# Feed-forward gate and up projections by seven products per 2×2 block: an fp32 trunk of two layers on one core

## The chip, the core and the metric

The kernel runs on one core of a Trainium2 chip. The metric is device time in microseconds (us), as the median of three runs; the kernel before takes 1412.47 us (1409.63 to 1412.63). The core's engines are TensorE (PE; its weight loads are shown as PEld), VectorE (DVE), ScalarE (ACT), GpSimd (POOL) and SyncE (SP), which here only issues DMA transfers. Each engine executes its own instructions in program order and waits for others at semaphores.

## The reference

The program is a trunk of two residual layers for 512 tokens of width 1024, all in fp32. Layer 0 mixes tokens by retention, layer 1 by stick-breaking attention, and each is followed by the same kind of feed-forward part, which is what the change is about:

```
def swiglu(h, w_in, w_out):
    gate, up = jnp.split(h @ w_in, 2, axis=-1)
    return (jax.nn.silu(gate) * up) @ w_out

def reference(x, ...):
    for i in range(DEPTH):                              # DEPTH = 2
        h = rms_norm(x, mix_norm[i])
        x = x + (retention(h, ...) if i % N_MIXERS == 0 else stick_breaking(h, ...))
        x = x + swiglu(rms_norm(x, ffn_norm[i]), ffn_w_in[i], ffn_w_out[i])
    return x
```

`w_in` is 1024 x 5632 (gate and up of 2816 each) and `w_out` 2816 x 1024, per layer.

## The kernel before

**Layout.** Channels lie on the 128 partitions and the 512 tokens along the free dimension: `x` is eight tiles of 128x512 (k = 0..7). To keep fp32 accuracy every operand is held as a pair of high and low part, and every product is three matmuls, high by high, low by high, high by low (`split3`, L131 to L133 of the profile). The normalisation's row factor is applied behind the product; only the gain is multiplied into `xh`, `xl` (`norm_in`, L141, L142).

**Weights.** All weights come in blocks of 128x1024 fp32 (512 KB). The class `Weights` loads a block by a DMA from SP into `raw` (three buffers, three ahead), ACT copies it to the high part `wh` (L72) and DVE subtracts that from it to get the low part `wl` (L73), two blocks ahead of TensorE. PE takes the blocks in the order of the program's steps.

**Feed-forward.** A layer has 22 hidden tiles f of 128 channels, in two halves of 11. Tiles 0 and 1 are computed first in four chunks as the x tiles arrive (`ffn_first`, `ch_chunk`); then the column of mean squares (`stats_col`, L164 to L168, which needs `sq`, a running sum that POOL adds, L158) and a row form of the factor (`stats_row`, L175, L178). `ffn_tile(f)` for f from 2 computes gate and up as 8 x 3 matmuls of 512 columns each, one weight block for each; `ffn_act` then does gate by row (L502) on DVE, Silu (L504) on ACT, up by row and by that (L506, L507) on DVE, and the split into `hh` (L138, ACT) and `hl` (L139, DVE). Behind each half `ffn_out_chunk` multiplies the hidden tiles by `ffn_out`, and `add_x` adds the result to x (L233).

**Order of work.** The steps are issued in program order on each engine; the loads and splits of blocks run ahead of the step that takes them. All matmul results lie in one ring of eight PSUM banks, tag `mm`.

Of the kernel before, what the change touches and what calls it, by code (L numbers as in the profile page):

```python
# [26 lines left out]
HALF = FF // P // 2  # L27


class Weights:  # L30
# [3 lines left out]
    def __init__(self, nc, raw, split, load_ahead, split_ahead):  # L34
        self.nc, self.raw, self.split = nc, raw, split
        self.aps, self.raws, self.parts = [], {}, {}
        self.n_load = self.n_split = self.n_take = 0
        self.load_ahead, self.split_ahead = load_ahead, split_ahead
        self.hooks = {}
        self.first = None  # L40

    def load(self, n):
        nc = self.nc
        while self.n_load < min(n + self.load_ahead, len(self.aps)):
            for hook in self.hooks.pop(self.n_load, ()):
                hook()
            ap = self.aps[self.n_load]
            t = self.raw.tile([P, 1024], F32, tag="raw", name=f"raw{self.n_load}")
            w = ap.shape[-1]
            if self.n_load == 0 and self.first:  # L50
                for half, (ready, _) in zip((slice(0, w // 2), slice(w // 2, w)), self.first):
                    ready()
                    nc.sync.dma_start(t[:, half], ap[:, half])
            else:
                nc.sync.dma_start(t[:, :w], ap)
            self.raws[self.n_load] = (t, w)
            self.n_load += 1

    def advance(self, n):
        nc = self.nc  # L60
        self.load(n)
        while self.n_split < min(n + self.split_ahead, self.n_load):
            t, w = self.raws.pop(self.n_split)
            h = self.split.tile([P, 1024], F32R, tag="wh", name=f"wh{self.n_split}")
            l = self.split.tile([P, 1024], F32R, tag="wl", name=f"wl{self.n_split}")
            parts = [slice(0, w)]
            if self.n_split == 0 and self.first:
                parts = [slice(0, w // 2), slice(w // 2, w)]
            for i, part in enumerate(parts):
                if len(parts) > 1:  # L70
                    self.first[i][1]()
                nc.scalar.activation(h[:, part], t[:, part], AF.Copy)  # L72
                nc.vector.tensor_tensor(l[:, part], t[:, part], h[:, part].bitcast(F32), ALU.subtract)  # L73
            self.parts[self.n_split] = (h, l, w)
            self.n_split += 1

    def take(self):
        n = self.n_take
        self.advance(n + 1)
        self.n_take += 1  # L80
        return self.parts.pop(n)
# [810 lines left out]
```

## Time and profile before

| | us |
|---|---|
| median of three runs (range) | 1412.47 (1409.63 to 1412.63) |
| the profiled execution's own time | 1406.76 |
| its span, first to last instruction | 1405.1 |
| PE busy in it | 1381.4 (98%) |
| DVE, ACT, POOL busy | 723.8, 511.7, 204.1 |
| feed-forward of layer 0, gate and up from f = 3 / output | 92.5 + 119.6 / 60.4 + 60.5 |
| stick-breaking stage | 269.2 |

The profile is one execution, 5.7 us below the median of the three timed runs. Stages were found by following PE's instructions in time; a busy share is of the stretch named. An instruction's duration on PE overlaps the next one's, so PE's rate is read from the distance of starts. The clock granted to PE was 0.998 of full speed over the span, the higher of its two levels (2.4 GHz) nearly throughout.

### The profile page before, as it was taken

To read this page: it belongs to the slowest core of one execution; us is meant where nothing else is said; L and a number is where in the kernel's file an instruction comes from. 1 tells how busy PE (TensorE), PEld (TensorE's weight loads), DVE (VectorE), ACT (ScalarE), POOL (GpSimd) and SP (SyncE) were. 2 spreads that over 40 slices of the span, in tenths; PEclk is the share of its full clock that TensorE was granted. 3 is DMA by queue.
4 is the path that set the end of the run, shared out by engine and by line. 5 is a ranking of instruction groups with operands and counts; after the bars stand their busy time and mean duration, and the time that the engine had idled before them with its cause. 6 is when DMAs were issued, how large, how long until landed. Compare 5 with 4: busy or idle time off the path is not lost.

```text
span 1405.1 us, 16161 instructions
## 1 busy us (share of the span) xinstructions
PE 1381.4 (98%) x6331; PEld 1144.6 (81%) x6331; DVE 723.8 (52%) x915; ACT 511.7 (36%) x768; POOL 204.1 (15%) x262
## 2 busy tenths in 40 slices
PE   9999999999999999999999999988999999999999
PEld 7888888888888888888888887766888888888887
DVE  6555345364374443344434357789994443344432
ACT  5243233332353232223333356667653322223221
POOL 3000000000020000000002245676830000000000
PEclk9999999999999999999999999999999999999999
DMA  6322222213232323333234344335223333333332
GB/s 233 97 83 83 90 75 90 91 61 104 76 90 90 100 92 98 101 92 103 87 113 137 99 120 123 89 92 148 76 74 94 103 88 98 99 104 91 90 109 71
DMA packets 41948, 138.96 MB, mean 99 GB/s; under 512 B 5008, under 2 KB 5264, under 8 KB 41872
## 3 DMA queue, kind: packets, MB, share of 16 engines
q1 hardware_dynamic: 41872, 137.93, 32.5%
q8 instruction: 49, 0.80, 0.2%
q14 instruction: 27, 0.22, 0.1%
HBM read 125.33 MB, written 4.19 MB: 92 GB/s over the span
## 4 chain that ended last, share of the span: by engine, by line
PE 90%; DVE 3%; POOL 3%; issue 2%; ACT 1%; DMA 1%; SPq 0%; POOLq 0%; DVEq 0%; ACTq 0%
PE mm L131 29%; PE mm L133 29%; PE mm L132 29%; PE mm L698 1%; POOL sn L657 1%; POOL qf L603 1%; POOL w L664 1%; DVE wl L73 1%; PE mm L649 1%; PE mm L677 1%; DVE sn L663 1%; PE mm L405 0%; PE mm L650 0%; POOL w L657 0%; DMA raw<-in_ret_tok_dram 0%
## 5 line engine op out<-in xcount | busy, mean ns | idle before, releaser
L72 ACT ACTIVATE wh<-raw 128x1024 fp32r<-128x1024 f32 (+2 forms) x233 | 243.1, 1044 | 702.6 <-PE mm L132 410.5
L73 DVE TENSOR_TENSOR wl<-raw,wh 128x1024 fp32r<-128x1024 f32 (+2 forms) x233 | 285.8, 1227 | 278.9 <-ACT wh L72 277.9
L131 PE MATMUL mm<-xh,wh 128*128 128x512 f32 x832 | 324.4, 390 | 0.0
L133 PE MATMUL mm<-xh,wl 128*128 128x512 f32 x832 | 323.8, 389 | 0.0
L132 PE MATMUL mm<-xl,wh 128*128 128x512 f32 x832 | 323.7, 389 | 0.0
L133 PEld LDWEIGHTS mm<-xh,wl 128*128 128x128 f32 x832 | 156.2, 188 | 32.8
L131 PEld LDWEIGHTS mm<-xh,wh 128*128 128x128 f32 x832 | 156.2, 188 | 32.2
L132 PEld LDWEIGHTS mm<-xl,wh 128*128 128x128 f32 x832 | 156.2, 188 | 32.2
L132 PE MATMUL mm<-wl,xh 128*128 128x512 f32 x448 | 175.0, 391 | 1.5 <-DVE wl L73 1.4
L131 PE MATMUL mm<-wh,xh 128*128 128x512 f32 x448 | 175.1, 393 | 0.0
L133 PE MATMUL mm<-wh,xl 128*128 128x512 f32 x448 | 175.0, 391 | 0.0
L131 PE MATMUL mm<-hh,wh 128*128 128x512 f32 (+1 forms) x363 | 140.5, 387 | 0.0
L133 PE MATMUL mm<-hh,wl 128*128 128x512 f32 (+1 forms) x363 | 139.8, 385 | 0.0
L132 PE MATMUL mm<-hl,wh 128*128 128x512 f32 (+1 forms) x363 | 138.5, 382 | 0.0
L132 PEld LDWEIGHTS mm<-wl,xh 128*128 128x128 f32 x448 | 84.3, 188 | 19.7 <-DVE wl L73 2.8
L158 POOL TENSOR_TENSOR sq<-sq,sqt 128x512 f32<-128x512 f32 x28 | 43.1, 1538 | 391.4 <-issue 293.9
L133 PEld LDWEIGHTS mm<-wh,xl 128*128 128x128 f32 x448 | 84.1, 188 | 17.5
L131 PEld LDWEIGHTS mm<-wh,xh 128*128 128x128 f32 x448 | 84.2, 188 | 16.9
L506 DVE TENSOR_TENSOR us<-mm,row 128x512 f32<-128x512 f32 x44 | 30.4, 691 | 124.9 <-PE mm L133 124.9
L233 DVE TENSOR_TENSOR x<-mm,x 128x512 f32<-128x512 f32 x87 | 59.4, 686 | 57.9 <-PE mm L133 57.8
L133 PEld LDWEIGHTS mm<-hh,wl 128*128 128x128 f32 x363 | 68.1, 188 | 15.0
L132 PEld LDWEIGHTS mm<-hl,wh 128*128 128x128 f32 x363 | 68.1, 188 | 14.4
(114 smaller groups left out, 1589.0 us busy)
## 6 DMA issues: line engine op xcount, KB each, us to landing
raw<-in_ffn_in_dram SPq DMA_DIRECT2D x88, 512.0 KB, 3.5
raw<-in_ffn_out_dram SPq DMA_DIRECT2D x32, 512.0 KB, 3.5
raw<-in_ret_tok_dram SPq DMA_DIRECT2D x31, 512.0 KB, 3.5
raw<-in_sb_in_dram SPq DMA_DIRECT2D x24, 512.0 KB, 3.5
raw<-in_ret_ch_dram SPq DMA_DIRECT2D x16, 512.0 KB, 3.6
raw<-in_ret_o_dram SPq DMA_DIRECT2D x16, 512.0 KB, 3.5
kk<-kt SPq DMA_DIRECT2D x32, 256.0 KB, 4.4
raw<-in_ffn_out_dram SPq DMA_DIRECT2D x16, 384.0 KB, 3.2
```

Of the source, the lines that this page charges most:

```text
L72: nc.scalar.activation(h[:, part], t[:, part], AF.Copy)
L73: nc.vector.tensor_tensor(l[:, part], t[:, part], h[:, part].bitcast(F32), ALU.subtract)
L131: nc.tensor.matmul(ps, ah, bh, start=start, stop=False)
L132: nc.tensor.matmul(ps, ah, bl, start=False, stop=False)
L133: nc.tensor.matmul(ps, al, bh, start=False, stop=stop)
L158: nc.gpsimd.tensor_tensor(state["sq"], state["sq"], t, ALU.add)
L233: nc.vector.tensor_tensor(x[m], bank, x[m], ALU.add)
L506: nc.vector.tensor_tensor(us, up, row, ALU.mult)
L603: nc.gpsimd.tensor_tensor(QF[which, g][:, t], ss, mhalf, ALU.pow)
L649: nc.tensor.matmul(bank[:, :n], qs[:, ts], kk[:, 0, :n], start=True, stop=False)
L657: nc.gpsimd.affine_select(out=t[:, ts], in_=t[:, ts], compare_op=ALU.is_gt, fill=fill, base=0, pattern=[[-1, P]], channel_multiplier=1)
L663: nc.vector.tensor_tensor_scan(d, d, d, 1.0, ALU.mult, ALU.bypass)
```

## The change

For f = 2 to 21 gate and up are computed in groups of two tiles, ten groups per layer. In a group the weights are taken as a 2x2 matrix of blocks (even or odd k by gate or up) and x as a 2x2 matrix (even or odd k by the two halves of the tokens, `H1`, `H2`). Winograd's form of Strassen's product then needs seven products in place of eight. Each product takes one 128x1024 block (plain or a sum of blocks) and is 4 x 2 x 3 = 24 matmuls of 256 columns (`product`).

* The sums on the weight side are made as follows: `t3` = w22 + w12 and `t1` = w11 + w12 by a second, accumulating DMA that POOL issues onto a block already loaded (L116); `t2` = t1 + w22 and `t4` = t2 + w21 by DVE (L129). Blocks have two rings, `RAWS` 3 and `GROUP_RAWS` 6; ACT makes the high parts up to four items ahead, DVE the low parts with three buffers.
* The sums on the x side (`ffn_sums`) are made once per layer for each pair of k: two ACT copies (L595), four DVE operations of 256 columns (L598 to L601), and the split into `sxh` and `sxl` (128x1024; L241, L242).
* On the output side one product seeds another's bank: ACT copies a bank to a bank (L673, L689) or to SBUF (`p7`, L685) and DVE adds `p7` into a bank (L690) or to SBUF (`up`, L697). The first product of the next group (`ffn_group_open`, w11) is computed in the middle of a group, behind its third product.
* The tiles go in three passes of 8, 8 and 6 (`PASSES`), each with its output stage. The row factor of `up` moves from the hidden tiles to the output (`ffn_add`, two DVE operations in place of one). `stats_col` stands behind the second chunk instead of the fourth. PSUM has two rings of four banks, `mm` and `sd`.
* In the stick-breaking stage `sn` gets a buffer of its own for each j, where it had a ring of three, and `w3` has two buffers, where it had three.

```diff
-    def ffn_tile(f):
-        def go():
-            gate, up = psum(), psum()
-            ch_tile(gate)
-            ...
-            ch_tile(up)
-            ...
-            ffn_act(f, gate, up)
+    def product(bank, name, start):
+        h, l, _ = W.take()
+        ...
+        for p in range(KT // 2):
+            xh, xl = ff["ops"][p][name]
+            for s in range(2):
+                out = bank[:, s * (S // 2) : (s + 1) * (S // 2)]
+                nc.tensor.matmul(out, h[:, p, s], xh, ...)
+                nc.tensor.matmul(out, h[:, p, s], xl, ...)
+                nc.tensor.matmul(out, l[:, p, s], xh, ...)
+    def ffn_group_open(f):
+        def go():
+            a = bank("mm")
+            product(a, "11", True)
+            if f == 2:
+                stats_row(lambda: bank("mm"), ff["t"])
+                for i in range(2):
+                    ffn_up(i, ff["first"][2 * i + 1], ffn_gate(ff["first"][2 * i], None), None)
+            b = bank("sd")
+            nc.scalar.activation(b, a, AF.Copy)
+            ff["next"] = {"a": a, "b": b}
+    def ffn_group(f, n):
+        def go():
+            g = ff["group"] = ff["next"] if n == 0 else ff["group"]
+            if n == 0:
+                t = bank("mm")
+                product(t, "s3", True)
+                nc.scalar.activation(g["p7"], t, AF.Copy)
+            elif n == 1:
+                product(g["b"], "s2", False)
+                nc.scalar.activation(g["d"], g["b"], AF.Copy)
+                nc.vector.tensor_tensor(g["c"], g["b"], g["p7"], ALU.add)
+            elif n == 2:
+                product(g["a"], "12", False)
+                g["gate"] = ffn_gate(g["a"], H1)
+            elif n == 3:
+                product(g["d"], "s1", False)
+                nc.vector.tensor_tensor(g["up"], g["d"], g["p7"], ALU.add)
+            elif n == 4:
+                product(g["c"], "22", False)
+                ffn_up(f, g["up"], ffn_gate(g["c"], H2), H2)
+            else:
+                product(g["d"], "s4", False)
+                ffn_up(f, g["d"], g["gate"], H1)
...
+                for n in range(6):
+                    step(ffn_group(f, n), *([entry] if n == 0 and not own else []))
+                    if n == 2 and following:
+                        step(ffn_group_open(f + 2))
...
+                nc.sync.dma_start(t[:, :w], aps[0])
+                for ap in aps[1:]:
+                    nc.gpsimd.dma_start(t[:, :w], ap, accum_op=ALU.add)
...
-                w = sb["t"].tile([P, n], F32, tag=f"w{j}", name="w", bufs=3)
-                r = sb["t"].tile([P, S], F32, tag="sn", name="sn", bufs=3)
+                w = sb["t"].tile([P, n], F32, tag=f"w{j}", name="w", bufs=3 - (j == 3))
+                r = sb["t"].tile([P, n], F32, tag=f"sn{j}", name="sn", bufs=1)
```

**What moves on DVE at the start of layer 0's feed-forward part.** Before, DVE's rows from the last x tile to the first gate are these (`ms` is the mean-square column, `wl` a block's low part):

```order
L142 SCALAR_TENSOR_TENSOR xl<-x_81,gains,xh 128x512
L73 TENSOR_TENSOR wl_3230<-raw_3197,wh_3229 128x1024
L73 TENSOR_TENSOR wl_3260<-raw_3227,wh_3259 128x1024
L73 TENSOR_TENSOR wl_3290<-raw_3257,wh_3289 128x1024
L166 TENSOR_SCALAR ms<-mm 128x4
L73 TENSOR_TENSOR wl_3331<-raw_3287,wh_3330 128x1024
L73 TENSOR_TENSOR wl_3379<-raw_3328,wh_3378 128x1024
L502 TENSOR_TENSOR gs<-mm,row 128x512
```

After the change 29 rows stand between the last `xl` and the first `gs`; the last twelve of them and the gates are:

```order
L600 SCALAR_TENSOR_TENSOR xsum<-xsum,xg 128x256
L160 TENSOR_TENSOR wl_3361<-raw_3295,wh_3309 128x1024
L601 SCALAR_TENSOR_TENSOR xsum<-xg,xsum 128x256
L129 TENSOR_TENSOR sum<-sum,rawg 128x1024
L242 TENSOR_TENSOR sxl<-xsum,sxh 128x1024
L129 TENSOR_TENSOR sum<-rawg 128x1024
L160 TENSOR_TENSOR wl_3404<-sum,wh_3359 128x1024
L129 TENSOR_TENSOR sum<-sum,rawg 128x1024
L160 TENSOR_TENSOR wl_3460<-rawg,wh_3402 128x1024
L642 TENSOR_TENSOR gs<-mm,row 128x512 x2
L657 TENSOR_TENSOR us<-mm,gs 128x512
```

The sums of x, the two weight sums of the first group and those of the second stand ahead of the first gate. ACT, at the same place, has the seed of the first group's bank (L673) between the two Silus (L646):

```order
L145 ACTIVATE wh_3458<-raw_3305 128x1024
L281 ACTIVATE row<-mm 128x512
L646 ACTIVATE gs<-gs 128x512
L673 ACTIVATE mm<-mm 128x512
L646 ACTIVATE gs<-gs 128x512
L241 ACTIVATE hh<-us 128x512
```

The seed can thus be made only after the first gate has left DVE.

**What moves on DVE inside the stage.** Before, DVE's rows for two tiles in layer 0 repeat this pattern of six for each tile:

```order
L73 TENSOR_TENSOR wl_3506<-raw_3460,wh_3505 128x1024
L139 TENSOR_TENSOR hl<-us,hh 128x512
L502 TENSOR_TENSOR gs<-mm,row 128x512
L73 TENSOR_TENSOR wl_3536<-raw_3503,wh_3535 128x1024
L506 TENSOR_TENSOR us<-mm,row 128x512
L507 TENSOR_TENSOR us<-us,sil 128x512
```

After the change one group of two tiles has 17 rows; twelve of them, from the seed of bank c on:

```order
L690 TENSOR_TENSOR mm<-mm,p_3724 128x512
L645 TENSOR_TENSOR gs<-mm,row 128x512
L160 TENSOR_TENSOR wl_3794<-sum,wh_3758 128x1024
L129 TENSOR_TENSOR sum<-rawg 128x1024
L160 TENSOR_TENSOR wl_3824<-rawg,wh_3792 128x1024
L697 TENSOR_TENSOR up<-mm,p_3724 128x512
L160 TENSOR_TENSOR wl_3854<-raw_3520,wh_3822 128x1024
L645 TENSOR_TENSOR gs<-mm,row 128x512
L160 TENSOR_TENSOR wl_3893<-sum,wh_3852 128x1024
L660 SCALAR_TENSOR_TENSOR us<-up,gs 128x512
L129 TENSOR_TENSOR sum<-sum,rawg 128x1024
L242 TENSOR_TENSOR hl<-us,hh 128x2x256
```

Per group that is seven low parts, two weight sums and eight operations of 512 columns, where two tiles had four low parts and eight operations.

## Rows read from the trace of the kernel before

**Rows 1.** The page's busy times by engine.

```profile
PE 1381.4 (98%) x6331; PEld 1144.6 (81%) x6331; DVE 723.8 (52%) x915; ACT 511.7 (36%) x768; POOL 204.1 (15%) x262
```

**Rows 2.** The chain that ended last, by engine.

```profile
PE 90%; DVE 3%; POOL 3%; issue 2%; ACT 1%; DMA 1%; SPq 0%; POOLq 0%; DVEq 0%; ACTq 0%
```

**Rows 3.** Busy times by stretch, granted clock, DMA share, GB/s.

```profile
core 0: us, PE busy (x) PEld busy (x) DVE busy (x) ACT busy (x) POOL busy (x), PEclk, DMA share, GB/s
408.80:431.50 22.70, 22.70 (x106) 18.88 (x104) 9.37 (x9) 7.46 (x9) 2.73 (x3) 1.00 0.38 115
437.40:529.90 92.50, 92.50 (x411) 76.61 (x409) 46.85 (x58) 30.37 (x39) 0.00 (x0) 1.00 0.31 95
...
590.40:710.00 119.60, 119.60 (x529) 99.00 (x529) 54.23 (x64) 35.44 (x43) 0.00 (x0) 1.00 0.32 99
...
770.50:1039.70 269.20, 251.39 (x1258) 207.99 (x1257) 202.88 (x277) 160.50 (x310) 153.87 (x214) 0.99 0.36 104
1039.70:1062.40 22.70, 22.70 (x107) 18.92 (x105) 13.85 (x12) 8.66 (x11) 6.93 (x4) 1.00 0.36 115
```

**Rows 4.** PE in time (start, us), first and last matmuls of 528 in the second half.

```profile
590.45 0.40 PE L131 MATMUL mm<-xh,wh 128*128 128x512 f32 x1
...
709.95 0.39 PE L133 MATMUL mm<-xh,wl 128*128 128x512 f32 x1
```

**Rows 5.** PE in time, matmuls of 256 columns near the end.

```profile
1389.15 0.28 PE L131 MATMUL mm<-hh,wh 128*128 128x256 f32 x1
...
1390.21 0.28 PE L131 MATMUL mm<-hh,wh 128*128 128x256 f32 x1
```

**Rows 6.** Instructions by line from 1341 to 1405 us (count, busy us, mean ns, idle before).

```profile
L131 PEld LDWEIGHTS mm<-hh,wh 128*128 128x128 f32 x99 | 18.6, 188 | 2.9
...
L526 DVE TENSOR_TENSOR x<-mm,x 128x256 f32<-128x256 f32 x2 | 0.8, 425 | 1.0 <-PE mm L133 1.0
```

**Rows 7.** The same view, 590.4 to 710 us.

```profile
L73 DVE TENSOR_TENSOR wl<-raw,wh 128x1024 fp32r<-128x1024 f32 x22 | 26.9, 1223 | 2.9 <-ACT wh L72 2.9
L72 ACT ACTIVATE wh<-raw 128x1024 fp32r<-128x1024 f32 x22 | 23.4, 1064 | 77.5 <-issue 38.6 <-PE mm L132 35.4 <-PE mm L133 3.4
L502 DVE TENSOR_TENSOR gs<-mm,row 128x512 f32<-128x512 f32 x11 | 7.6, 692 | 25.5 <-PE mm L133 25.5
...
L504 ACT ACTIVATE sil<-gs 128x512 f32<-128x512 f32 x11 | 6.8, 614 | 0.0
L138 ACT ACTIVATE hh<-us 128x512 fp32r<-128x512 f32 x10 | 6.3, 634 | 6.4 <-DVE us L507 6.4
```

**Rows 8.** The page's DMA issues, median us to landing.

```profile
raw<-in_ffn_in_dram SPq DMA_DIRECT2D x88, 512.0 KB, 3.5
```

**Rows 9.** DVE in time at the start of layer 0's feed-forward part.

```profile
412.25 1.54 DVE L73 TENSOR_TENSOR wl<-raw,wh 128x1024 fp32r<-128x1024 f32 x1
...
415.41 1.21 DVE L73 TENSOR_TENSOR wl<-raw,wh 128x1024 fp32r<-128x1024 f32 x1
```

**Rows 10.** POOL in time, the same place.

```profile
413.55 1.39 POOL L158 TENSOR_TENSOR sq<-sq,sqt 128x512 f32<-128x512 f32 x1 [0.84 <-ACT sqt L157]
```

**Rows 11.** PE in time, the same place.

```profile
430.65 0.95 PE L164 MATMUL mm<-ones,sq 128*128 128x1 f32 x8
431.45 0.49 PE L131 MATMUL mm<-xh,wh 128*128 128x512 f32 x1
...
437.04 0.60 PE L175 MATMUL mm<-ident,rstd 128*128 128x128 f32 x4
437.39 0.48 PE L131 MATMUL mm<-xh,wh 128*128 128x512 f32 x1
```

**Rows 12.** ACT in time, after layer 1's row factor.

```profile
1068.86 0.58 ACT L178 ACTIVATE row<-mm 128x512 f32<-128x512 f32 x1
1069.46 1.28 ACT L504 ACT_TABLE_LOAD   x1
```

**Rows 13.** Instructions by line, ACT from 770.5 to 1039.7 us.

```profile
L653 ACT ACTIVATE sn<-mm 128x512 f32<-128x512 f32 x16 | 9.6, 603 | 8.3 <-POOL w L664 8.3
```

More of the change, by code (lines that the diff above doesn't have):

```diff
@@ L52, in load @@
                     ready()
-                    nc.sync.dma_start(t[:, half], ap[:, half])
+                    nc.sync.dma_start(t[:, half], aps[0][:, half])
             else:
-                nc.sync.dma_start(t[:, :w], ap)
-            self.raws[self.n_load] = (t, w)
-            self.n_load += 1
-    def advance(self, n):
-        nc = self.nc
[L61 to L75, printed above, removed]
+                nc.sync.dma_start(t[:, :w], aps[0])
@@ new lines, in load, with sum_to @@
+                for ap in aps[1:]:
+                    nc.gpsimd.dma_start(t[:, :w], ap, accum_op=ALU.add)
+            self.tiles["load", self.n_load] = (t, w)
+            self.ring[kind].append(("load", self.n_load))
+            self.n_load += 1
+    def sum_to(self, n):
+        while self.n_sum < min(n, len(self.items)):
+            src, parts = self.items[self.n_sum]
+            if parts:
+                if any(name not in self.tiles for name in parts):
+                    return
+                (a, w), (b, _) = (self.use(name) for name in parts)
+                t = self.group_pool.tile([P, 1024], F32, tag="sum", name="sum", bufs=3)
+                self.nc.vector.tensor_tensor(t, a, b, ALU.add)
+                self.tiles[src] = (t, w)
+            self.n_sum += 1
@@ new lines, in high_to @@
+    def high_to(self, n):
+        while self.n_h < min(n, self.n_sum):
+            src, _ = self.items[self.n_h]
+            if src not in self.tiles:
+                return
+            t, w = self.tiles[src]
+            h = self.split.tile([P, 1024], F32R, tag="wh", name=f"wh{self.n_h}", bufs=4)
+            self.h[self.n_h] = h
+            self.n_h += 1
+            if self.n_h == 1 and self.first:
+                self.low_to(1)
+            else:
+                self.nc.scalar.activation(h[:, :w], t[:, :w], AF.Copy)
@@ L118, in trunk @@
     nc.scalar.activation(warm, ones, AF.Silu)
-    zero = cp.tile([P, P], F32, name="zero")
+    zero = st.tile([P, P], F32, tag="sqt", name="zero")
     nc.vector.memset(zero, 0.0)
-    start = psr.tile([P, S], F32, tag="mm", name="start")
+    start = bank("mm")
     for _ in range(11):
@@ L247, in run @@
     def run():
-        W.aps = list(order)
+        for entry in order:
+            W.add(entry)
         W.hooks = load_hooks
-        W.n_load = W.n_split = W.n_take = 0
         for fn in steps:
             fn()
-        assert W.n_take == len(order)
+        assert W.n_take == len(W.items)
         order.clear()
```

282 lines of the change are left out of this document (211 added, 71 removed).

## The prediction

> **What bounds the kernel now.** I read the page's busy times first: PE is busy for 1381.4 of 1405.1 us, and no other engine for more than 52% [rows 1]. PE's busy time alone does not prove a bound, since matmuls are pipelined, so I went to the chain that ended last: 90% of it is PE [rows 2]. The table of stretches then shows where there is room beside PE [rows 3]. In the gate and up stage (590.4 to 710 us) PE has no gap, DVE is busy for 54.23 of 119.6 us, ACT for 35.44, POOL for nothing, and DMA has a share of 0.32. What shortens PE's list there shortens the kernel, as long as the others keep up. The stick-breaking stage is different: PE is busy for 251.39 of 269.2 us, beside a DVE and a POOL that work three quarters and more than half of it.
>
> PE's rate I read from starts. In the second half of layer 0, 528 matmuls of 512 columns start between 590.45 and 709.95 us [rows 4], 119.50 us over 527 distances: 226.8 ns each. Two tiles, 96 matmuls, take 21.77 us.
>
> **PE's side of the change.** A group becomes 7 x 24 = 168 matmuls of 256 columns. Before has such matmuls only at its very end: nine distances between 1389.15 and 1390.21 us [rows 5], 117.8 ns each, every one with a weight load of its own, as the new ones have. PEld lists such a load at 188 ns [rows 6], longer than the distance, so loads overlap one another and the stream. A group is then 168 x 0.1178 = 19.79 us, 1.98 less than before; the gain is not the full eighth, 2.72, because half the columns cost 52% of the time. Twenty groups give **-39.6 us**. If the loads were not hidden at this width, 188 ns would be the distance, the group 31.6 us; the rows of 256 columns speak against that, though they show only a short stretch with other operands.
>
> The Trainium skill, "TensorE: Matmul & The Clock Gate", section "Back-to-back issue gap", gives 518 cycles for 512 columns and 262 for 256, as isolated gaps, and warns that in a stream the weight load shares in setting the distance. By its cycles at 2.4 GHz, an estimate, a group would go from 20.7 to 18.3 us and the twenty would give -48 us. The trace disagrees at both widths (226.8 and 117.8 ns against 216 and 109), and the sum goes by the trace.
>
> **DVE in a group.** Seven low parts and two weight sums, all of 1024 columns; the low part takes 1.223 us [rows 7], and the sum has the same form. Eight operations of 512 columns at 0.692 us [rows 7]. That is 9 x 1.223 + 8 x 0.692 = 16.5 us, 84% of 19.79. Going down the rows shown, the tightest place is `up`, which reads bank d after product s1 and must be gone before s4 writes d: one product (2.83 us) for a low part in progress (1.22) and `up` (0.69), so it holds by 0.9 us. The low parts run more than 2 us ahead of the product that takes them. I cost DVE at **nothing**, under the cover of 3.3 us per group; without the cover every us of DVE per group costs 20.
>
> **ACT in a group.** Seven high parts at 1.064, three copies of 512 columns at about 0.6 (the row factor's copy took 0.58 [rows 12]), two Silus at 0.614, two splits at 0.634 [rows 7]: 11.7 us of 19.79. The seeds wait at most one high part. Nothing.
>
> **DMA in a group.** At 99 GB/s the 16 engines show a share of 0.32 [rows 3], 309 GB/s when busy, so one 512 KB block (0.524 MB) takes 1.70 us of all of them. A group loads five plain blocks, 8.5 us, and two accumulating ones. No row of before has an accumulating transfer. Bounds: below, a plain block, 1.70 us; above, none from the trace. Two of them bind when they exceed (19.79 - 8.5)/2 = 5.65 us each, 3.3 times a plain block. The latency of a plain block is 3.5 us [rows 8]; the items run about ten products (28 us) ahead inside a pass, so latency is covered even at several times that. I take them below 5.65, as they are nearest to the plain block, and so nothing; the other case is a rival.
>
> **The start of each feed-forward part** costs something. In layer 0, `stats_col` and the transposes keep their cost on PE: 0.8 us from 430.65 to 431.45 and 0.35 from 437.04 [rows 11]. New is that PE has first product w11 (2.83 us), then s3 (2.83), and then s2, which needs the seed of bank b. s3 ends at 431.45 + 2.83 + 0.35 + 2.83 = 437.5. The seed stands behind the first gate on DVE. DVE leaves the last `xl` at 415.41 [rows 9]; one `xsum` stands ahead of that and 29 rows behind it: altogether sixteen of 256 columns, priced at 0.425 [rows 6], and thirteen of 1024 (four `sxl`, five low parts, four weight sums) at 1.223: 22.7 us. Then the gate (0.69), its Silu (0.61) and the seed (0.58): 440.0, so 2.5 us late at least. DVE also waits for ACT: two of the four `sxl` stand directly behind the last `xsum`, and wait for ACT's `sxh` (1.06 each [rows 7]); the most, if all four waited for it and for two copies of 0.6, is 9 us. I take 2.3, hence **+5** for layer 0 (2.5 to 11.5). In layer 1 DVE carries 13.85 us of older work into the same stretch, not 9.37 [rows 3], 4.5 more; some of it falls into those waits, so I add 3: **+8** (2.5 to 16). A table load of 1.28 us stands between row and Silu there [rows 12], while DVE is still busy, so it is hidden. The earlier `stats_col` needs `sq`, whose last addition ends at 414.94 [rows 10], before the second chunk does, at 419.7 (408.8 + 48 x 0.2268); nothing in layer 0.
>
> **The rest.** The output stages keep their 264 matmuls per half. The second DVE operation per output tile has room there; the last one stands on the tail, **+0.4** (0.425 [rows 6]). In the stick-breaking stage ACT waited 8.3 us for POOL at `sn` [rows 13]; a buffer for each j can loosen that, `w3` with two can tighten it. PE's idle 17.8 us there bounds the gain, but the waits sit off PE's chain for the most part; I take 0, with 3 to either side.
>
> **Sum.** 1406.8 (the profiled execution) - 39.6 + 13 + 0.4 = 1380.6 us. The median stood 5.7 above the profiled execution, so **1386 us**.
>
> **The rivals.**
>
> *The start is covered* (a). If the 256-column operations cost half of what I took and ACT stays ahead, the seed comes at 437 to 439 and PE waits under 2 us in each layer: 11 less, **1375**. For it: PE has 22 us of first-chunk matmuls to cover DVE, and parts of the sums can start before the last x. Against: the row order puts gates behind all of it, and counted work alone passes s3's end.
>
> *DVE becomes the bound in the groups* (c). Beside POOL's additions the low part took 1.54 us, not 1.22 [rows 9]. If issuing the accumulating transfers slowed DVE all the time, nine rows at 1.54 and eight at 0.692 give 19.4 us: still under 19.79, yet without the slack that `up` and the low parts need, some 0.5 to 1 us of waits per group, 10 to 20 us: **1396 to 1406**. The point from which it decides is 1.3 us per group (26.2 us of gain over 20). For it: DVE at 84% in strict order, with deadlines of a product's length. Against: POOL only issues two transfers per group, it does not add.
>
> Of that contention the Trainium skill, "SBUF — State Buffer", section "Who interferes with whom", says that a DVE operation with two SBUF inputs is held up by a GpSimd instruction that reads SBUF, and that writing descriptors is not a read. The slow low parts beside POOL's additions agree with the first half (1.54 against 1.22 us); no run here shows the second, and by it this rival comes only from order, not from duration.
>
> *The accumulating transfers bind* (b), the case on the other side. At 4.5 times a plain block (7.65 us) a group's DMA takes 8.5 + 15.3 = 23.8 us, 4.0 more than PE needs: 80 us more than forecast, **1466**. Level with before is 6.3 us each (21.1 us per group), 3.7 times. For it: each has to read what it adds to, beside five plain blocks on the same engines, and one POOL queue issues all. Against: half of the engines' time is free, and three times a plain block would still fit.
>
> *Weight loads are not hidden at 256 columns in this stage* (d): 11.8 us more per group, **1622**; the 117.8 ns speak against it.
>
> **How the numbers follow.** The forecast case (groups at PE's rate, a stall at each start; 1378 to 1396) has 0.50, (a) 0.17, (c) 0.18, (b) 0.10, (d) 0.02, and 0.03 is for what I do not see. A measurement here can tell about 0.2%, 2.8 us. Slower than that takes nearly all of (b) and (d) and a fifth of (c) with the rest: 0.15; within it 0.04, from the upper end of (c) and the level point of (b); faster 0.81. The range from 1370 to 1409 holds the forecast, (a) and most of (c), eight in ten.
>
> **What would show it.** Right: 256-column matmuls in the groups about 118 ns apart, groups of 19.8 us without gaps, DVE near 84% there, DMA share under 0.8, a PE wait of 3 to 10 us before the first s2 (released by ACT's seed) in each layer. Wrong: PE idle at low parts (L160) or at `up`'s bank in every group (c); L160 or L145 waiting for DMA, with accumulating transfers beyond 5.65 us of the engines (b); distances near 188 ns (d); or no idle before s2 (a).

## The result and the profile after

The changed kernel takes 1418.37 us (1416.86 to 1423.22) against 1410.51 us for the kernel before in the same session: ratio 1.0057, interval 1.0039 to 1.0075. It is slower by 0.6%, outside the forecast range. Its profiled execution has a span of 1421.4 us, 16.3 above that of before. That is more than the 7.9 us between the medians: the profile is of the longest of the six timed executions (1423.22 us), and that of before lies below its median, so what is split up below is the two profiles and not the medians.

From the page of the changed kernel: busy times, queues (packets, MB, share of 16 engines), the chain by engine, and the issues of the blocks for gate and up, plain ones from SP and accumulating ones from POOL (KB, median us to landing).

```profile
PE 1362.4 (96%) x7756; PEld 1194.9 (84%) x7756; DVE 892.8 (63%) x1116; ACT 620.7 (44%) x912; POOL 235.9 (17%) x302
...
q1 hardware_dynamic: 44752, 148.42, 32.7%
q0 software_dynamic: 5760, 20.97, 8.6%
...
PE 14%; DMA 3%; DVE 2%; issue 0%; DVEq 0%; POOLq 0%; SPq 0%
...
rawg<-in_ffn_in_dram SPq DMA_DIRECT2D x60, 512.0 KB, 3.7
...
rawg<-in_ffn_in_dram POOLq DMA_DIRECT2D x20, 512.0 KB, 7.6
raw<-in_ffn_in_dram POOLq DMA_DIRECT2D x20, 512.0 KB, 7.1
```

Against [rows 1], PE is busy for 19 us less, yet the span is longer: PE now has gaps. The chain by engine could be followed back for a fifth of the span only, where [rows 2] had nearly all of it, so it says little here; stretches and waits have to do. The stretches of the changed kernel (columns as in [rows 3]): start, first, second and third pass of layer 0, stick-breaking, start and first pass of layer 1. The first passes are counted from their second product (s3) on.

```profile
410.80:436.60 25.80, 25.80 (x131) 21.95 (x130) 18.95 (x29) 14.62 (x19) 6.88 (x7) 1.00 0.83 253
436.60:506.50 69.90, 61.27 (x485) 60.51 (x484) 49.91 (x56) 34.30 (x45) 3.60 (x5) 0.95 0.56 143
...
550.40:634.40 84.00, 80.20 (x673) 79.61 (x673) 60.56 (x67) 43.25 (x54) 5.17 (x6) 1.00 0.60 158
678.30:738.60 60.30, 60.11 (x505) 59.90 (x504) 42.43 (x47) 31.77 (x41) 1.72 (x2) 1.00 0.33 89
771.60:1053.00 281.40, 257.97 (x1258) 213.65 (x1257) 205.56 (x282) 161.83 (x311) 151.25 (x214) 0.96 0.38 110
...
1083.50:1149.60 66.10, 61.13 (x484) 60.37 (x483) 47.02 (x54) 35.29 (x45) 3.42 (x4) 0.95 0.52 139
```

Three things are to be seen. The third pass, 504 matmuls in 60.3 us, runs as forecast and has no gap. The first passes have 5 to 9 us without PE work and a granted clock of 0.95; the second has 4 us of gaps. And the stick-breaking stage takes 281.4 us where [rows 3] had 269.2, at a clock of 0.96 instead of 0.99.

Against the forecast's span (1405.1 - 26.2 = 1378.9) 42.5 us are missing. By stretches: layer 0's feed-forward part took 360.8 us (410.8 to 771.6) against 361.7 before, where -14.8 was forecast: 13.9 missing. Layer 1's took 368.4 (1053.0 to the end) against 365.3, where -11.4 was forecast: 14.5 missing. Stick-breaking: 12.2. The rest, 2.0, lies in the retention layer's first 50 us; its cause was not looked for.

Who PE and DVE waited for after 405 us, in the changed kernel (total us, times, longest), from PE's waits and from DVE's:

```profile
PE mm L621 <- DVE up L697: 14.8, 13, 2.2
...
PE mm L621 <- ACT mm L673: 4.1, 1, 4.1
```

```profile
engine line waited for: us in total, times, longest us
DVE sum L129 <- DMA rawg<-in_ffn_in_dram: 61.8, 14, 5.8
```

DVE stood still for 61.8 us at its weight sums, fourteen times, for a block in transfer, and PE thirteen times for `up`. One of these places, in the second pass of layer 0, from the timelines of DVE, SP, POOL and PE, with PE's first row after its wait at the end:

```profile
574.87 1.22 DVE L160 TENSOR_TENSOR wl<-rawg,wh 128x1024 fp32r<-128x1024 f32 x1
...
576.16 0.33 SPq L114 DMA_DIRECT2D rawg<-in_ffn_in_dram  x1
...
580.23 0.86 POOL L116 DMA_DIRECT2D rawg<-in_ffn_in_dram  x1 [17.77 <-ACT wh L145]
...
582.63 1.22 DVE L160 TENSOR_TENSOR wl<-sum,wh 128x1024 fp32r<-128x1024 f32 x1
589.47 1.23 DVE L129 TENSOR_TENSOR sum<-rawg 128x1024 f32<-128x1024 f32 x1 [5.62 <-DMA rawg<-in_ffn_in_dram]
...
591.75 0.68 DVE L697 TENSOR_TENSOR up<-mm,p 128x512 f32<-128x512 f32 x1
...
592.58 0.36 PE L621 MATMUL mm<-sxh,wh 128*128 128x256 f32 x1 [2.00 <-DVE up L697]
```

DVE's low part frees a block at 576.1; SP loads the next `t1` block into it at 576.16; POOL issues the accumulating transfer onto it at 580.23; DVE reaches the sum `t2` at 583.85, when its last low part ends, and can start it only at 589.47. The block needs 13.3 us from free slot to both transfers landed (3.5 for the first, 0.6 until POOL issues, 9.2 for the second), and DVE's order gives it 7.7. The sum's other block, w22, is no earlier here. SP issued it at 580.42, beside the accumulating transfer, and it took 8.8 us to land, until 589.2; plain blocks had a median of 3.7. The two transfers (KB, us to landing):

```profile
rawg<-in_ffn_in_dram POOLq DMA_DIRECT2D x1, 512.0 KB, 9.2
rawg<-in_ffn_in_dram SPq DMA_DIRECT2D x1, 512.0 KB, 8.8
```

By the landings in the trace, eleven of the seventeen waits of over 2 us at `t2` (the three that the profile puts down to issue among them) end with the accumulating transfer, and six with w22, three of these within 0.25 us of it. Behind the sum stand a low part and `up`; product s4 needs the bank that `up` reads, and PE waits 2.00 us. The sum's own product is not yet due.

### The profile page after: what moved, and what is told of

Read it like the earlier page. It is cut to its first block, busy times and chain, and to the rows that moved or that the text cites. A ratio compares the mean times of both kernels' runs of the same rounds, so it can differ in the third digit from the quotient of the medians.

```text
span 1421.4 us, 19714 instructions
## 1 busy us (share of the span) xinstructions
PE 1362.4 (96%) x7756; PEld 1194.9 (84%) x7756; DVE 892.8 (63%) x1116; ACT 620.7 (44%) x912; POOL 235.9 (17%) x302
## 5 line engine op out<-in xcount | busy, mean ns | idle before, releaser
L145 ACT ACTIVATE wh<-raw 128x1024 fp32r<-128x1024 f32 (+1 forms) x191 | 199.1, 1043 | 437.2 <-PE mm L235 198.2
L160 DVE TENSOR_TENSOR wl<-raw,wh 128x1024 fp32r<-128x1024 f32 (+1 forms) x191 | 237.5, 1245 | 186.6 <-PE mm L235 93.1
L621 PE MATMUL mm<-sxh,wh 128*128 128x256 f32 x640 | 183.4, 286 | 21.2 <-DVE up L697 14.8
L624 PE MATMUL mm<-sxh,wl 128*128 128x256 f32 x640 | 181.4, 283 | 0.0
L623 PE MATMUL mm<-sxl,wh 128*128 128x256 f32 x640 | 181.3, 283 | 0.0
L621 PEld LDWEIGHTS mm<-sxh,wh 128*128 128x128 f32 x640 | 123.3, 193 | 24.1 <-issue 8.4
L624 PE MATMUL mm<-xh,wl 128*128 128x256 f32 x480 | 135.8, 283 | 1.7 <-DVE wl L160 1.7
L621 PE MATMUL mm<-xh,wh 128*128 128x256 f32 x480 | 135.8, 283 | 0.0
L623 PE MATMUL mm<-xl,wh 128*128 128x256 f32 x480 | 135.7, 283 | 0.0
L624 PEld LDWEIGHTS mm<-sxh,wl 128*128 128x128 f32 x640 | 123.2, 192 | 0.0
```

The source lines that it names most:

```text
L145: self.nc.scalar.activation(h[:, :w], t[:, :w], AF.Copy)
L160: nc.vector.tensor_tensor(l[:, :w], t[:, :w], h[:, :w].bitcast(F32), ALU.subtract)
L621: nc.tensor.matmul(out, h[:, p, s], xh, start=start and p == 0 and s == 0, stop=False, skip_group_check=True)
L623: nc.tensor.matmul(out, h[:, p, s], xl, start=False, stop=False, skip_group_check=True)
L624: nc.tensor.matmul(out, l[:, p, s], xh, start=False, stop=last, skip_group_check=True)
```

## The experiments

Theory A, after this reading: DVE's sums stand in its strict order and wait for the accumulating transfers, and `up` behind them comes late for PE. (That a plain block can be the last to land, as shown above, is not part of it.) B is the rival that the expectations set against it, C and F are about the stick-breaking stage (buffer counts, order), E about additions by POOL; each expectation says what it makes of the run.

Fourteen further kernels ran. "Wait at the sums" is what the profile puts down as DVE's wait for DMA at its weight sums after 405 us. The change has three more waits there, 9.3 us together, that the profile puts down to issue; the other runs with a second transfer and sums on DVE have 2.0 to 11.6 us of these.

| run | us | ratio to before (interval) | wait at the sums, us |
|---|---|---|---|
| the change | 1418.4 | 1.0057 (1.0039 to 1.0075) | 61.8 |
| e1 sums two products later | 1415.1 | 1.0022 (1.0005 to 1.0039) | 62.9 |
| e2 no accumulating transfer | 1389.1 | 0.9848 (0.9831 to 0.9864) | 9.4 (longest 1.2) |
| e3 seed first | 1413.1 | 1.0012 (0.9997 to 1.0027) | 63.9 |
| e4 before, new sn and w3 counts | 1411.4 | 0.9997 (0.9988 to 1.0007) | (no such sums) |
| e5 t3, t1 by POOL | 1403.0 | 0.9937 (0.9922 to 0.9952) | none |
| e6 second transfer plain | 1395.9 | 0.9894 (0.9871 to 0.9916) | 35.6 |
| e7 t2, t4 by POOL | 1405.8 | 0.9958 (0.9946 to 0.9970) | none on DVE |
| e8 old sn and w3 counts | 1415.0 | 1.0025 (1.0013 to 1.0037) | 48.7 |
| e9 = e5 and e8 | 1395.0 | 0.9892 (0.9874 to 0.9910) | none |
| e10 seven group blocks | 1399.0 | 0.9917 (0.9893 to 0.9941) | none |
| e11 = e10, seed first | 1388.0 | 0.9838 (0.9823 to 0.9852) | none |
| e12 three high parts | 1426.2 | 1.0109 (1.0092 to 1.0126) | 66.1 |
| e13 = e11, all sums kept | 1387.0 | 0.9842 (0.9825 to 0.9860) | none |
| e14 = e9, seed first | 1395.0 | 0.9894 (0.9880 to 0.9907) | none |

### e1: the sums two products later

```diff
-        self.sum_to(n + 6)
+        self.sum_to(n + 4)
```

> The changed kernel with one number changed: the weight sums t2 and t4 (L129) stand two products later in DVE's order (four items ahead, not six). Theory A (in the groups PE loses time because a sum stands in DVE's order before its accumulating transfer has landed; DVE then waits up to 5.6 us, up (L697) is late, s4 waits, and the clock falls behind the wait): DVE's waits of L129 for DMA fall from 31 us in layer 0 to under 8, PE's waits for up from 14.9 us over both layers to under 5, and the time from 1418 us to 1402 to 1409. Rival B (DVE's own load of 84% in strict order makes up late, whatever the transfers do): PE still waits 10 us or more for up, and the time stays within 4 us of 1418.

Measured: 1415.1 us; DVE's waits at the sums 62.9 us, PE's for `up` 13.6. Neither number moved, and the time is the one that the expectation gave to rival B. But the edit did not do what theory A needed: in the two groups from 570 to 616 us DVE's rows stand in the same order as in the change, so the sum still reaches its transfer too early. The run is thus no test of either.

### e2: no accumulating transfer

```diff
-                for ap in aps[1:]:
-                    nc.gpsimd.dma_start(t[:, :w], ap, accum_op=ALU.add)
```

> The changed kernel without the accumulating transfers: t3 is then w22 alone and t1 w11 alone, everything else stands. Theory A: the waits of L129 for DMA nearly vanish, PE's waits for up with them, and the time falls from 1418 to 1400 to 1408; the start of each feed-forward part keeps most of its stall. Rival B: DVE has the same rows, so PE still waits 10 us or more for up, and the time stays within 4 us of 1418. A third way, that the accumulating transfers cost the engines so much that all other loads are late, would also show as a DMA share that falls from 0.56 to below 0.45 in the first pass, with plain loads landing in 3.5 us and not 3.7.

Measured: 1389.1 us, 29 less than the change. First pass, second pass and stick-breaking:

```profile
436.00:492.50 56.50, 56.49 (x477) 56.28 (x476) 45.72 (x52) 32.55 (x45) 0.00 (x0) 1.00 0.39 129
536.50:616.30 79.80, 79.80 (x673) 79.77 (x672) 61.93 (x67) 43.03 (x55) 0.00 (x0) 1.00 0.38 126
753.20:1030.40 277.20, 254.32 (x1257) 211.11 (x1256) 205.56 (x279) 161.89 (x311) 155.83 (x214) 0.97 0.38 113
```

The passes have no gap and full clock, 56.5 and 79.8 us where the change had 69.9 and 84.0. PE waited for nothing in layer 0, not at the start either, with the same rows on DVE. Theory A stands, rival B falls. The time is below A's 1400, because the start's stall hangs on these transfers too, which I had not expected, and about 4 us of the 29 are the stick-breaking stage's. The third way of the expectation is not ruled out by this run: the DMA share fell to 0.39 in the first pass, and plain blocks landed in 3.4 to 3.5 us. It falls with e10 and e13 below, which keep the transfers and a share of 0.61 in a second pass without gaps.

### e3: the seed ahead of the gates

```diff
-                ff["first"] = [bank("sd") for _ in range(4)]
+                ff["first"] = [bank(tag) for tag in ("mm", "mm", "sd", "sd")]
...
+            b = bank("sd")
+            nc.scalar.activation(b, a, AF.Copy)
             if f == 2:
                 stats_row(...)
                 ...
-            b = bank("sd")
-            nc.scalar.activation(b, a, AF.Copy)
```

A seed that goes to the bank of the statistics is not added to here, so a part of one group's sum is left out per layer; no instruction is missing.

> The changed kernel with the first group's seed (L673) ahead of the row factor and the two gates of f = 0 and 1; for that the four first banks are spread over both rings and the statistics share one bank. If the prediction's step on the start is right (s2 waits for a seed behind DVE's backlog), the 4.2 us before s2 in layer 0 shrink to about 2.4 (then the low part of t2 decides, 439.9 us), the half-clock stretch behind it goes, and the time falls by 3 to 4 us to about 1414. Rival: the low parts are as late as the seed, so the wait only changes its name, and the time stays within 2 us of 1418.

Measured: 1413.1 us, 5 less. The wait before s2 in layer 0 is gone; PE's only waits there are those for `up`:

```profile
PE mm L621 <- DVE up L698: 8.2, 5, 3.4
```

So the seed's place was the wait. Together with e2: the seed stood behind the gates, the gates behind DVE's first sum, and the sum behind its transfer.

### e4, e8 and e12: the stick-breaking stage

e4 is the kernel before with the new counts of `sn` and `w3`; e8 the changed kernel with the old ones (for which the fourth high-part buffer outside the feed-forward parts has to go); e12 the changed kernel with three high-part buffers and the new counts.

```diff
-            h = self.split.tile([P, 1024], F32R, tag="wh", ..., bufs=4)
+            h = self.split.tile([P, 1024], F32R, tag="wh", ..., bufs=3)
...
-        W.ahead = 2
+        W.ahead = 1
```

> The kernel before with nothing but the two buffer counts of the stick-breaking stage changed as in the change: sn one buffer for each j in place of a ring of three, w3 two buffers in place of three. Theory C (these buffers cost the 12 us that the stage grew from 269 to 281): the stage grows by 8 to 13 us, the granted clock in it falls from 0.99 to about 0.96, and the time goes from 1410.5 to 1418 to 1424. Rival D (the growth comes from what else moved: the later x from the output stage, the order of the splits, the two PSUM rings): within 3 us of 1410.5.

> The changed kernel with sn as a ring of three and three buffers for w3 again (the room comes from the fourth high-part buffer, which then exists in the feed-forward parts alone). In this kernel these counts change the order in which the stage's instructions are arranged (18 of POOL's rows and 42 of DVE's stand elsewhere than before; with the old counts none of POOL's and 10 of DVE's). Theory F (the stage's 12 us come from that order): the stage takes 269 to 273 us, its granted clock is back at 0.98 to 0.99, and the time is 1407 to 1411. Rival: the stage stays at 277 to 282, the time within 4 us of 1418.

> The changed kernel with three high-part buffers and ACT one item less ahead in the feed-forward parts, and nothing else; the group ring keeps six blocks, sn and w3 the new counts. It parts the two edits of the run with seven blocks and the two of the run with old counts. If the seventh block is what ended DVE's waits for DMA: here DVE waits as in the changed kernel (over 40 us over both layers), PE for up over 8 us. If ACT's lesser lead (and the order of DVE that follows from it) ended them: waits under 15 us and 1398 to 1403 us. The stick-breaking stage, whose rows this edit alone puts back in the order of before: 269 to 275 us if the order makes its time, 278 to 282 if sn and w3 do. With the first answers to both, 1408 to 1414 us.

The stage in e4, e8 and e12:

```profile
772.70:1044.30 271.60, 251.82 (x1257) 208.44 (x1256) 203.63 (x277) 159.97 (x310) 153.05 (x214) 0.99 0.36 103
```

```profile
772.90:1045.60 272.70, 253.43 (x1257) 209.25 (x1257) 205.57 (x281) 162.09 (x312) 152.47 (x216) 0.98 0.39 115
```

```profile
779.20:1053.90 274.70, 253.79 (x1258) 210.24 (x1257) 206.97 (x281) 163.00 (x314) 152.92 (x216) 0.98 0.39 115
```

271.6, 272.7 and 274.7 us, where the change has 281.4 and before 269.2. Theory C falls with e4: the counts of `sn` and `w3` cost 2.4 us at most (271.6 - 269.2).

What the kernels with the long stage share is the fourth high-part buffer in the pool that this stage uses too. By PE's starts the stage takes 277.2 to 281.4 us in the seven that have it there (the change, e1, e2, e3, e5, e6, e7) and 271.9 to 274.8 in the seven changed kernels that have not (e8 to e14). It goes with another order of the stage: in the traces some 40 of POOL's 214 rows there leave the order of before in the change, and one to seven in e4, e8 and e12 (the 18 and none of e8's expectation are counts in the built programs). Theory F (the order) fits; that the order and not the buffer itself costs was not tried apart.

e8's time, 1415 us, was above the 1407 to 1411 expected: its stage gave 9 us, but in its profile PE waited 5.6 us for the seed in the first pass of layer 0, and the granted clock there was 0.90, which took back some of it; why the seed was later I did not test.

e12 took 1426.2 us where 1408 to 1414 was expected: with three high-part buffers and ACT's lesser lead PE waits 21.9 us for `up` instead of 14.8 and 9.1 for the seed instead of 4.1. Its waits at the sums are as in the change.

### e5, e6 and e7: what of the transfer costs, and whom

```diff
# e5: four blocks per group; sums where they are first needed
+            self.items += [(t3, ((pool, t3, b22, t1), (pool, t1, self.w11, t1))),
+                           (t2, ((dve, t2, t1, b22),)), (b21, ())]
# e6
-                    nc.gpsimd.dma_start(t[:, :w], ap, accum_op=ALU.add)
+                    nc.gpsimd.dma_start(t[:, :w], ap)
# e7
-                self.nc.vector.tensor_tensor(t, a, b, ALU.add)
+                self.nc.gpsimd.tensor_tensor(t, a, b, ALU.add)
```

> The changed kernel without accumulating transfers, with the same result: each of the four weight blocks of a group is loaded once by SP, and POOL adds t3 = w22 + w12 into a tile and t1 = w11 + w12 in place (two additions of 128x1024 per group); DVE keeps t2 and t4. Theory A (the accumulating transfers are what costs; without them the groups run as in the run without accumulation): groups at 119 ns per matmul with PE waits under 3 us per layer, and 1386 to 1396 us. Rival E (POOL's additions slow DVE's two-input rows from 1.22 to 1.54 us and make its strict order late in turn): low parts above 1.35 us in the mean, PE waits for up or the low parts of 10 us or more, 1400 to 1412.

> The changed kernel with the second transfer of t3 and t1 as a plain one that overwrites (so t3 = w12, t1 = w12): the same queue, issue, order and bytes, and no addition. If the addition itself is the cost (3.06 us of all engines and 7 to 7.6 us to landing, against 1.64 and 3.7 for a plain block): landing falls to 4 to 5 us, DVE's waits of L129 fall from 61 us to under 20 over both layers, 1390 to 1400 us. If it is the chain (a slot comes free, SP loads, POOL issues a second transfer after the first has landed): landing hardly changes the waits, DVE still waits over 35 us, 1407 us or more.

> The changed kernel with its accumulating transfers, but t2 and t4 added by POOL in place of DVE. If the loss is in DVE's strict order (a sum waits for its transfer, and the low parts and up behind it wait too, though the sum's own product is still far off): PE's waits for up fall from 14.9 us to under 5, and the time to 1390 to 1402. If the sums' data are late for their own products: PE waits as long as now, only at L160 or L145 of s2 and 22, and the time stays above 1410.

e6, from its page:

```profile
q0 software_dynamic: 5760, 20.97, 4.5%
...
rawg<-in_ffn_in_dram POOLq DMA_DIRECT2D x20, 512.0 KB, 5.1
raw<-in_ffn_in_dram POOLq DMA_DIRECT2D x20, 512.0 KB, 4.3
```

Of 1393.0 us, 4.5% over 40 transfers is 1.57 us of the 16 engines each; with addition it was 8.6% of 1421.4, 3.06 us. Landing falls from 7.6 and 7.1 to 5.1 and 4.3 us. The time falls by 22 of e2's 29 us, as the expectation had it for the addition, but DVE still waits 35.6 us, as it had it for the chain: the addition's length is most of the cost, and the chain of two transfers through one slot the rest.

e7 leaves the transfers and moves the waiting to POOL: no wait for `up` is left in either layer, and the time falls by 13 us (1405.8, above the 1390 to 1402 expected), though the low parts became slower beside POOL's additions (up to 1.83 us in the mean, by kind). So the loss in the groups is in DVE's strict order. What remained was the start, 4.4 us at the seed and 4.6 us at a low part.

e5 keeps the result and needs no accumulating transfer: 1403.0 us, faster than before. It lies above e2 and my range and in rival E's, but not on the path that E named: PE waited 2.1 us for low parts in layer 0 and for `up` not at all, and the second and third pass run at 79.7 and 59.8 us, as in e2. Of the 16 us between the two profiles 11 lie in the first passes and 3.5 in the stick-breaking stage. The low parts are slower, as E had it: 1.34 us in the mean, the slowest kind in e5's layer 0 (out<-in, count, busy, mean ns):

```profile
L170 DVE TENSOR_TENSOR wl<-sum,wh 128x1024 fp32r<-128x1024 f32 x29 | 42.2, 1456 | 8.7 <-PE mm L246 6.3 <-PE mm L634 2.0 <-ACT wh L155 0.4
```

In the change their mean is 1.22 us there.

### e9, e10, e11, e13, e14: towards a version that is faster

> The two edits that helped, together: the weight sums t3 and t1 by POOL with no accumulating transfer (1403 us alone) and the old buffer counts of the stick-breaking stage (1415 us alone, against 1418). If the two are independent, as theories A and F have it: the stage near 272 us, the groups as in the run with POOL's sums, and 1396 to 1400 us, ratio 0.989 to 0.992 to the kernel before. Rival: the gain of the old counts was a matter of this execution's clock, and the two together stay at 1401 to 1405.

1395.0 us, 1 us below the range: the gains of e5 (15.4 us) and e8 (3.4) alone make 18.8 us, and together they gave 23.4. That e8's own time was held up at the seed would account for it, but was not tried.

```diff
# e10
-    RAWS, GROUP_RAWS = 3, 6
+    RAWS, GROUP_RAWS = 3, 7
-            h = ... bufs=4)
+            h = ... bufs=3)
-        W.ahead = 2
+        W.ahead = 1
```

> The changed kernel with its accumulating transfers and seven block buffers in the group ring in place of six; the room comes from the fourth high-part buffer, so ACT runs one item less ahead. The stick-breaking stage is then arranged as in the run with the old counts (all of POOL's rows as before), so it is compared with that run (1415 us). If the slot is what makes t1 late (its first load can start only when a block of the group before last has been split): DVE's waits of L129 for DMA fall from about 49 us in both layers there to under 20, PE's waits for up from 11.8 us to under 4, and the time to 1398 to 1406. If the landing time of the addition itself is: waits over 30 us, and 1412 us or more.

DVE's largest wait and its wait at the sums in e10, and the latter in e12, which differs by the seventh block alone:

```profile
DVE wl L160 <- ACT wh L145: 146.4, 143, 4.2
...
DVE sum L129 <- issue: 5.8, 1, 5.8
```

```profile
DVE sum L129 <- DMA rawg<-in_ffn_in_dram: 66.1, 16, 6.0
```

DVE waits for DMA at the sums for 66.1 us in e12 and not in e10, where one wait of 5.8 us is left at the first sum of layer 0; 27 us lie between the two kernels. The accumulating transfers take much the same share of the engines (8.7% against 8.4%); they start earlier. What e10 has left at the start, from PE's waits:

```profile
PE mm L621 <- ACT mm L673: 9.9, 2, 5.1
```

> The run with seven group blocks (1399 us) plus the first group's seed ahead of the row factor and gates (the bank it goes to gets one full matmul first, in the first two groups, so that the seed is added to). In that run the only large PE waits left in the feed-forward parts are for this seed, 4.8 and 5.1 us, each with 6.8 us at half clock behind it. If the start is a matter of the seed's place alone: both waits fall under 1.5 us, the half-clock stretches at 446 and 1074 us go, and the time falls by 12 to 17 us to 1382 to 1387. Rival: without the seed the low part of t2 or the split sums of x (sxh) hold PE almost as long, at half clock too: 1393 to 1399.

The part of a sum that e3 leaves out is left out here too. 1388.0 us, 1 us above the range: the seed's two waits are gone, and 11 us with them.

> The run with seven group blocks and the seed first, with all results kept: in that run one of the first group's banks (the one of the statistics) still lost a seed; here both banks that had not been filled by matmuls get one full matmul each before a seed goes there (two matmuls of 512 columns per layer, 0.5 us). If those lost sums had no part in the time, as all its instructions were there: 1386 to 1390 us, ratio 0.982 to 0.986, PE waits of the feed-forward parts under 5 us. Rival: the matmul into the statistics' bank waits for ACT's row factor on PE and gives back 2 us or more per layer: 1391 to 1396.

e13 adds one matmul of 512 columns into each of the two banks, so that the seed is added there too; nothing is left out: 1387.0 us, 0.9842 of the kernel before (0.9825 to 0.9860), the fastest version here with all results. First and second pass of layer 0, stick-breaking, first pass of layer 1, and PE's largest wait in the feed-forward parts:

```profile
436.00:496.00 60.00, 58.49 (x486) 57.59 (x485) 52.73 (x58) 35.32 (x47) 4.32 (x5) 1.00 0.68 178
539.00:619.00 80.00, 80.00 (x675) 79.95 (x674) 63.19 (x67) 42.92 (x54) 5.18 (x6) 1.00 0.61 166
...
756.00:1030.00 274.00, 253.19 (x1255) 210.11 (x1254) 206.35 (x281) 162.44 (x313) 152.34 (x216) 0.98 0.39 116
...
1058.00:1120.00 62.00, 59.23 (x475) 58.07 (x474) 52.05 (x57) 36.06 (x48) 3.42 (x4) 0.97 0.56 159
```

```profile
PE mm L624 <- DVE wl L160: 2.6, 3, 1.3
```

The second pass is gapless: 675 PE instructions in 80.00 us, 118.5 ns each.

> POOL's weight sums and the old buffer counts (1395 us) with the seed first, results kept, six blocks. If the accumulating transfers cost nothing once they have lead, and POOL's additions cost by slowing DVE (low parts of up to 3.4 us beside them in the first pass): the seed brings little here (its wait is 0.5 us in layer 0), 1391 to 1396 us, behind the version with seven blocks. If the start is the same matter in both: 1383 to 1388.

1395.0 us, as e9: without accumulating transfers the seed has nothing to gain, and POOL's additions cost 8 us against seven blocks. The start's cost belonged to the transfers.

## Why the prediction was wrong

**The step that failed** is the sentence on latency: "the items run about ten products (28 us) ahead inside a pass, so latency is covered even at several times that". The lead is not set by how far ahead the items are asked for, but by when a block of the ring of six comes free and by where DVE's sum stands: 7.7 us in the place shown. And the need is not one latency but two in a row with a hand-over through POOL, 13.3 us, and a plain block issued beside the second took 8.8 us there and not 3.5. With one block more (e10) the waits in the groups are gone. I had stepped through DVE's order for the low parts' deadlines, and priced a sum at its 1.22 us without asking when its inputs arrive.

**PE's rate** was right: 117.8 ns forecast, 118.5 in the gapless pass of e13, so 19.9 us per group and 37 us for twenty, not 39.6. The Trainium skill's "TensorE: Matmul & The Clock Gate" ("Back-to-back issue gap") gives 262 cycles for 256 columns, 109 ns at 2.4 GHz as an estimate; that is not reached.

**DVE and ACT in a group**: 84% forecast; 63.19 of 80.00 us, 79%, in e13. Nothing there binds once the sums do not wait. Rival (c) named the mechanism, order against deadlines, and 10 to 20 us, but gave it to slower low parts; these took 1.217 to 1.220 us in the changed kernel's layer 0, and it was the sums.

**DMA's capacity** (rival b): 3.06 us of the engines per accumulating transfer, under the bound of 5.65; the DMA share is 0.56 and 0.60 in the change's first two passes and 0.68 and 0.61 in e13's. Over a group it does not bind. But the transfers come in bursts, with a share of 0.81 from 580 to 590 us in the change, where DVE waited. I had looked for the cost in the engines' time over a group, and it was in the time to landing.

**The start**: +5 and +8 forecast. In layer 0 PE waited 4.06 us, in order: POOL issues the accumulating transfer; DVE's first sum starts after 4.44 us of waiting (the profile names no releaser; without the transfer, in e2, the stall is gone); the gates; the seed; s2.

```profile
415.21 1.06 POOL L116 DMA_DIRECT2D rawg<-in_ffn_in_dram  x1 [0.20 <-issue]
...
424.58 1.23 DVE L129 TENSOR_TENSOR sum<-rawg 128x1024 f32<-128x1024 f32 x1 [4.44 <-issue]
...
442.15 1.28 DVE L642 TENSOR_TENSOR gs<-mm,row 128x512 f32<-128x512 f32 x2
...
443.40 0.58 ACT L673 ACTIVATE mm<-mm 128x512 f32<-128x512 f32 x1
...
444.03 0.38 PE L621 MATMUL mm<-sxh,wh 128*128 128x256 f32 x1 [4.06 <-ACT mm L673]
```

In layer 0 the number was right and half the cause: the seed's place behind the gates counts (e3), but DVE's backlog alone does not reach s2 (e2). In layer 1 the forecast path did not occur: PE did not wait for the seed there, but 2.7 us at 1058 for DVE's x and 1.7 us at 1088.7 for a low part. The clock added its part, in the stretches of PE's wait and behind it:

```profile
440.00:444.00 4.00, 0.00 (x0) 0.00 (x0) 3.90 (x5) 1.14 (x3) 0.00 (x0) 1.00 0.36 76
444.00:448.00 4.00, 3.97 (x20) 3.97 (x21) 2.64 (x4) 3.11 (x5) 0.86 (x1) 0.58 0.66 227
448.00:452.00 4.00, 4.00 (x35) 4.00 (x35) 2.87 (x4) 2.10 (x3) 0.86 (x1) 1.00 0.97 156
```

In the 4 us behind the wait the granted clock is 0.58, and PE gets through 20 matmuls instead of 35; then it is full again. Over the first pass, at 0.95 in 69.9 us, that makes 3.5 us, and the starts agree: 37 matmuls stand 212 ns apart in the mean and not 118.5.

**The stick-breaking stage**: 0 with 3 to either side, measured +12.2, a second term that was mis-sized. I took its order as nearly that of before and priced the buffer counts only; the counts cost 2.4 us at most (e4), and the rest goes with the fourth high-part buffer (e8, e12), which I had not priced.

**Tail and output stages**: the output stages have no gap, as forecast. The tail is longer than the +0.4 forecast: from the end of PE's last matmul to the end of the program the changed kernel takes 4.9 us and the one before 3.1. The forecast counted one of the added DVE operations there; the last three output pieces need six operations on DVE, one behind the other (1415.2 to 1418.6 us), where before had three.

## What to carry to other kernels

Before costing a producer at nothing, follow one buffer: when it comes free, how many transfers in a row must land in it, and where the first reader stands in its engine's order. A reader in strict order charges its wait to everything behind it, whose deadlines may be much closer than its own; one more buffer was worth 27 us between e12 and e10. And when a change adds a buffer to a pool that other stages share, compare those stages' order too.

## What the chip showed that I had not expected

In the change an accumulating transfer of 512 KB took 3.06 us of the 16 engines, against 1.57 for a plain one on the same queue (e6) and 1.64 from SP, and landed after 7.1 to 7.6 us against 4.3 to 5.1 and 3.7.

A low part can take 2.6 times its length beside an addition on POOL. In e9, from POOL's and DVE's timelines:

```profile
447.48 2.38 POOL L139 TENSOR_TENSOR rawg<-raw,rawg 128x1024 f32<-128x1024 f32 x1
...
447.79 3.15 DVE L173 TENSOR_TENSOR wl<-raw,wh 128x1024 fp32r<-128x1024 f32 x1 [2.04 <-PE mm L637]
450.87 1.21 DVE L173 TENSOR_TENSOR wl<-rawg,wh 128x1024 fp32r<-128x1024 f32 x1
```

The second low part, after the addition has ended, takes 1.21 us. The Trainium skill, "SBUF — State Buffer", section "Who interferes with whom", says that a two-input DVE operation is held up by a GpSimd instruction that reads SBUF; these rows agree. That descriptor generation does not do this to such an operation, which the section gives as inferred, agrees with the changed kernel, whose low parts kept 1.217 to 1.220 us in the mean in layer 0 beside POOL's issues.

PE's waits in the first passes could bring a stretch at the lower of its clock's two levels, 1.2 GHz, but not each did. Behind the 4.06 us wait shown above, in which PE had done nothing, 0.58 was granted over 4 us. From 460 to 470 and from 480 to 490 us PE was idle for about the same time, and the clock fell in the second only:

```profile
460.00:470.00 10.00, 7.91 (x67) 7.94 (x68) 10.00 (x13) 5.23 (x7) 0.00 (x0) 1.00 0.41 118
...
480.00:490.00 10.00, 7.78 (x54) 7.61 (x53) 8.61 (x10) 3.82 (x5) 0.00 (x0) 0.83 0.33 106
```

In the first pass of layer 0 the gaps are 8.6 us and the clock added 3.5; in e13, without the long wait, the gaps are 1.5 us and the clock is full. In layer 1 e13 still shows 0.97, with no single wait above 1.3 us.
